# Low parts of weights started earlier and accumulated from HBM, and a top-128 search that runs on into the attention

## The chip, the cores and the metric

The kernel runs on one NeuronCore of a Trainium2 chip. The metric is the device time of one execution in microseconds. TensorE, VectorE (DVE in the profile), ScalarE (ACT), GpSimd (POOL) and SyncE (SP, which here only issues DMAs) have a queue of their own each; what one queue holds runs in order, and engines wait for each other and for DMAs by semaphores.

## The reference

Two blocks work on 512 tokens of width 1024, all in float32. The first is one layer of sparse attention: a projection of the normalized tokens to 3,432 columns, three branches over eight heads (compressed, selected and windowed keys, mixed by gates) and one branch over another eight heads that attends to the 128 best keys of an indexer:

```python
logits = jnp.einsum('bthd,bsd->bths', qi_b, ki) * (IDX_DIM ** -0.5)
score = jnp.einsum('bths,bth->bts', jax.nn.relu(logits), wi_b).astype(jnp.float32)
score = jnp.where(key_pos[None, None, :] <= t[None, :, None], score, NEG)
_, idx = lax.top_k(score, topk)            # topk = 128
```

The compressed keys come from `hid = silu(flat @ w1 + b1)` over blocks of 32 tokens. The second block has two layers; each is a mixer (a gated linear recurrence and latent attention side by side) and a feed-forward, both with a modulation that depends on a condition vector:

```python
mod = (c @ w_ada + b_ada)[:, None, :]
sh_m, sc_m, g_m, sh_f, sc_f, g_f = jnp.split(mod, 6, axis=-1)
h = rms_norm_2(x) * (1 + sc_m) + sh_m
proj = h @ w_in
...
x = x + g_m * (y @ w_out)
h = rms_norm_2(x) * (1 + sc_f) + sh_f
gate, up = jnp.split(h @ w_ffn_in, 2, axis=-1)
x = x + g_f * ((jax.nn.silu(gate) * up) @ w_ffn_out)
```

## The kernel before

Every large product is taken in the fast float32r format with two parts per operand. A weight `raw` is rounded to a high part `wh`; the low part is `wl = raw - wh`; the activations are split in the same way, and a product is three matmuls, high by high, high by low and low by high (`proj_T`, L103). So a matmul with `wl` needs the low part in SBUF.

The weights come in chunks of 128 x 1024 or fewer, in the order of a list `plan` that is written out by hand (from L296). `load_chunk` (L172) issues the load of the next chunk into one of three buffers `raw` on SyncE's queue. `split_chunk` (L185) makes the two parts. ScalarE makes `wh`. The low part is made in one of two ways, by the engine that the plan names. With `DV` VectorE subtracts. With `GP` ScalarE writes the negative rounded weight into `wl`, and a DMA issued by GpSimd adds `raw` to it (L203):

```python
act(lo[:, :n], raw[:, :n], scale=-1.0)
yield 1
nc.gpsimd.dma_start(lo[:, :n].bitcast(F32), raw[:, :n], accum_op=ALU.add)
```

`take` (L221) hands a chunk to the matmuls and starts `run_ahead` (L211), which splits up to `ahead[0]` chunks beyond it (two, at places one or none) and loads one more. There are three buffers each of `raw`, `wh` and `wl`.

The rest of the program is written as small generators that are stepped by `tick`, once for each 640 ns of estimated TensorE time, so that the operations of side jobs are emitted between the matmuls. On engines named by `order(...)` the program order is kept; in the first block up to the attention and in much of the second block that is VectorE, at places others too; in the attention it is none.

The stages are: x and the weights E (indexer columns); kv tiles, C, A, Bq and Dv (keys, queries, values), with the compression (`cmp_step`, L710), whose weights `cw1` are chunks of the plan that aren't split; the gate columns `z` (L822); the attention over 26 units (from L1089), in which the second half of `z` and the first output chunks `wo1` are woven; then, twice, mixer (`w2`, `uqr`, `uqk`, `wo2`) and feed-forward (`ffi`, `ffo`).

`best_keys` (L590) finds the 128 best keys of a token: 16 rounds of MAX8 and MATCH_REPLACE8 on VectorE for each of three query tiles (256, 384 and 512 wide); the loop at L827 ticks until every side job, these rounds too, has been emitted.

The modulation sums run on VectorE: `w_ada` comes in tiles of 128 x 512 (256 KB) and is multiplied with `c_bc` and summed along the row. `ada_first(8)` runs in the attention, `ada_first(0, 1)` beside the output projection (L1257), `ada_steps` (L1844) in the first layer's mixer and feed-forward. `enter` (L1329) starts a mixer or a feed-forward: it multiplies with unnormalized activations first, and corrects by a shift for which `shifts` (L1384) sums `raw` times the shift on VectorE.

Of the kernel before, what the change touches and what calls it, by code (L numbers as in the profile page):

```python
# [29 lines left out]
AR = 4  # L30
TICK = 640.0
# [8 lines left out]
def hybrid_kernel(ctx: ExitStack, tc: tile.TileContext, a: dict, out: bass.AP):  # L40
# [85 lines left out]
    DV, GP = nc.vector, nc.gpsimd  # L126
# [42 lines left out]
    plan = []  # L169
    loaded, ready, count = {}, {}, [0, 0, 0]  # L170

    def load_chunk(beside=None):  # L172
        i = count[0]
        if i < len(plan):
            key, l, o, n, _ = plan[i]
            raw = wpool.tile([128, 1024], F32, tag="raw", name=name("raw"), bufs=3)
            for c in (0, n // 2) if beside else (0,):
                m = n // 2 if beside else n
                nc.sync.dma_start(raw[:, c:c + m], (a[key] if l is None else a[key][l])[:, o + c:o + c + m])
                if beside:  # L180
                    beside.pop(0)()
            loaded[i] = raw
            count[0] += 1

    def split_chunk(i):  # L185
        n, e = plan[i][3:]
        raw = loaded.pop(i)
        if e is None:
            ready[i] = None, None, raw
            return  # L190
        h = wpool.tile([128, 1024], F32R, tag="wh", name=name("wh"), bufs=3)
        lo = wpool.tile([128, 1024], F32R, tag="wl", name=name("wl"), bufs=3)
        ready[i] = h, lo, raw
        if i == 0:
            for p_ in (slice(0, n // 2), slice(n // 2, n)):
                act(h[:, p_], raw[:, p_])
                tt(lo[:, p_], raw[:, p_], h[:, p_].bitcast(F32), ALU.subtract, e)
            return
        act(h[:, :n], raw[:, :n])
        if e is GP:  # L200
            act(lo[:, :n], raw[:, :n], scale=-1.0)
            yield 1
            nc.gpsimd.dma_start(lo[:, :n].bitcast(F32), raw[:, :n], accum_op=ALU.add)  # L203
        else:
            yield 2
            tt(lo[:, :n], raw[:, :n], h[:, :n].bitcast(F32), ALU.subtract, e)

    splitting = []
    ahead = [2]

    def run_ahead(i):  # L211

        yield 1
        while count[1] <= min(i + ahead[0], len(plan) - 1):
            k = count[1]
            count[1] += 1
            yield from split_chunk(k)
        if count[0] <= i + 3:
            load_chunk()

    def take(key, l, o, n):  # L221
# [6 lines left out]
        while count[0] <= i:  # L228
            load_chunk()
        while count[1] <= i:  # L230
            count[1] += 1
            finish(go(split_chunk(count[1] - 1)))
# [66 lines left out]
    def plan_n(key, cw=None, es=(DV, GP, DV, GP)):  # L299
        C = WD[key]  # L300
        for c in range(4):
            plan1(off[key] + c * 2 * C, 2 * C, es[c])
            if cw is not None:
                plan.append(("cw1", cw, c * 1024, 1024, None))
# [21 lines left out]
    for l in range(L2):  # L326
        def w2_(k, e=None):
            chunks("w2", l, 3584 + k * 1024, 1024, 1, e)

        w2_(0), w2_(1)  # L330
        for k in range(4):
            chunks("w2", l, k * 896, 896, 1, DV if k % 2 else GP)
        for p_ in range(4):
            if p_:
                w2_(2 * p_, GP), w2_(2 * p_ + 1, GP)
            if p_ == 2:
                chunks("uqr", l, 0, 1024, 1)
            if p_ == EP:
                w2_(16 + EG)
            for k in range(2):  # L340
                w2_(8 + 2 * p_ + k, DV if p_ == 2 else GP)
            for m in GB[p_]:
                if m == KD - 1:
                    chunks("uqk", l, 0, 1024)
# [3 lines left out]
        chunks("wo2", l, 3072, 1024, 5)  # L348
        for c0, n in SEGS:
            for k in range(2 * n):  # L350
                chunks("ffi", l, (2 * c0 + k) * 1024, 1024, 1, GP if c0 == 0 and 2 <= k < 5 else DV)
# [9 lines left out]
    next(xs0)  # L361
    next(xs0)
    load_chunk()
    for _ in xs0:
        pass
    nc.sync.dma_start(ident, a["cst"][:, 0:128])
# [196 lines left out]
    sco = pP.tile([128, 1152], F32, name="sco")  # L563

    def post_scores():
        for t in range(1, NT):
            W = 128 * (t + 1)
            sc = sco[:, (0, 0, 256, 640)[t]:(0, 256, 640, 1152)[t]]
# [16 lines left out]
            if t == 1:  # L585
                go(best_keys())

    masks = {}
# [120 lines left out]

    def cmp_step(s, pk):  # L710
# [3 lines left out]
        def step_(c):  # L714
# [4 lines left out]
            w = take("cw1", s, c * 1024, 1024)[2]  # L719
            for i in range(8):  # L720
# [1543 lines left out]
```

## Time and profile before

| what | value |
|---|---|
| median of 3 runs | 1773.9 us (1771.15 to 1777.37) |
| the profiled execution, its own time | 1770.79 us |
| span in the profile, first to last instruction | 1769.0 us |
| mean granted TensorE clock | 0.986 |
| TensorE busy | 95% |
| VectorE, ScalarE, GpSimd busy | 62%, 54%, 22% |
| accumulating DMAs (`wl` from `raw`) | 78 |

A page row gives the busy time of an engine, not the time in which it is at its peak. The waits name who released an engine last. The granted clock is the share of TensorE's full clock in a stretch.

### The profile page before, as it was taken

What the parts mean: (1) busy time and instruction counts of PE and PEld (TensorE: products, weight loads), DVE (VectorE), ACT (ScalarE), POOL (GpSimd) and SP (SyncE); (2) the same over time, 40 slices, a digit from 0 to 9 for tenths busy, and PEclk for the clock granted to TensorE, in tenths of its full rate; (3) what the DMA queues carried; (4) which work ended last, traced back from release to release, by engine and by line L of the source; (5) the groups of instructions that cost most, each with busy time, mean ns of one, the idle gap of its engine ahead of it and who ended that gap; (6) DMA issues with size and microseconds to landing.
All of it is one profiled execution on the core that took longest, in us unless ns stands there. A gap on an engine that the chain in (4) does not pass through costs nothing.

```text
span 1769.0 us, 22764 instructions
## 1 busy us (share of the span) xinstructions
PE 1687.9 (95%) x8122; PEld 1389.5 (79%) x8124; DVE 1103.6 (62%) x2048; ACT 958.2 (54%) x1729; POOL 381.1 (22%) x429
## 2 busy tenths in 40 slices
PE   6979899989998999999999999999999999999998
PEld 5868677667776788888888888887788888888887
DVE  5767788768689876746555546657676733333335
ACT  5558787975766786442222224887885532222223
POOL 3236344531225244100000000235243100000000
PEclk9989999999999999999999999999999999999999
DMA  6546643165787822366457443564422343333322
GB/s 199 148 125 140 150 108 84 48 177 134 189 256 209 236 49 70 98 184 226 155 190 236 149 132 94 146 146 126 124 60 72 97 129 96 96 95 98 100 86 74
DMA packets 84976, 235.91 MB, mean 133 GB/s; under 512 B 10368, under 2 KB 13056, under 8 KB 84864
## 3 DMA queue, kind: packets, MB, share of 16 engines
q1 hardware_dynamic: 73600, 194.82, 35.5%
q0 software_dynamic: 11264, 39.65, 12.1%
q8 instruction: 64, 1.05, 0.2%
q14 instruction: 48, 0.39, 0.1%
HBM read 192.69 MB, written 2.10 MB: 110 GB/s over the span
## 4 chain that ended last, share of the span: by engine, by line
PE 65%; DVE 10%; issue 9%; DMA 8%; ACT 6%; POOL 3%; SPq 0%; POOLq 0%; DVEq 0%; ACTq 0%
PE mm L84 38%; PE s L84 20%; PE o L84 3%; DMA wl<-raw 3%; DMA ada<-in_ada_dram 3%; DVE ada L1850 2%; DMA raw<-in_w_dram 2%; PE pt L930 1%; ACT p L71 1%; PE pt L2017 1%; PE pt L84 1%; DVE wl L74 1%; DVE xc L1534 1%; ACT L71 1%; DVE xl L1622 0%
## 5 line engine op out<-in xcount | busy, mean ns | idle before, releaser
L71 ACT ACTIVATE wh<-raw 128x1024 fp32r<-128x1024 f32 (+3 forms) x257 | 263.3, 1026 | 578.6 <-PE mm L84 361.7
L84 PE MATMUL mm<-hh,wh 128*128 128x512 f32 x1408 | 444.9, 393 | 3.6 <-DVE z L74 3.4
L84 PEld LDWEIGHTS mm<-hh,wh 128*128 128x128 f32 x1408 | 265.3, 189 | 58.4 <-DVE z L74 3.5
L84 PE MATMUL mm<-hh,wl 128*128 128x512 f32 x736 | 290.1, 394 | 4.6 <-DMA wl<-raw 4.5
L74 DVE TENSOR_TENSOR wl<-raw,wh 128x1024 fp32r<-128x1024 f32 (+3 forms) x179 | 213.8, 1196 | 115.9 <-ACT wh L71 113.5
L84 PE MATMUL s<-hh,wh 128*128 128x512 f32 x688 | 213.8, 390 | 0.0
L74 POOL TENSOR_TENSOR nv<-nv,pwr 128x4 f32<-128x4 f32 (+1 forms) x6 | 7.4, 1234 | 776.7 <-DVE nv L1321 432.7
L84 PEld LDWEIGHTS mm<-hh,wl 128*128 128x128 f32 x736 | 139.4, 189 | 35.3 <-DMA wl<-raw 6.5
L84 PEld LDWEIGHTS s<-hh,wh 128*128 128x128 f32 x688 | 129.4, 188 | 26.6
L84 PE MATMUL s<-hh,wl 128*128 128x512 f32 x352 | 137.8, 392 | 2.7 <-DMA wl<-raw 2.7
L84 PE MATMUL mm<-uh,wh 128*128 128x512 f32 (+1 forms) x364 | 139.2, 382 | 0.0
L84 PE MATMUL mm<-ul,wh 128*128 128x512 f32 (+1 forms) x364 | 139.0, 382 | 0.0
L84 PE MATMUL mm<-uh,wl 128*128 128x512 f32 (+1 forms) x364 | 139.0, 382 | 0.0
L203 POOL DMA_DIRECT2D wl<-raw x78 | 68.9, 887 | 254.4 <-ACT wl L71 214.8
L1850 DVE SCALAR_TENSOR_TENSOR ada<-ada,c_bc 128x512 f32<-128x512 f32 x160 | 115.8, 756 | 7.2 <-DMA ada<-in_ada_dram 7.2
L74 DVE TENSOR_TENSOR sg<-s,sg 128x512 f32<-128x512 f32 x42 | 29.1, 692 | 116.4 <-PE s L84 116.4
L71 ACT ACTIVATE p<-s,st 128x512 f32<-128x512 f32 (+3 forms) x160 | 83.9, 527 | 23.7 <-DVE st L1994 16.9
L1769 DVE SCALAR_TENSOR_TENSOR x<-mm,mod,x 128x512 f32<-128x512 f32 x46 | 34.5, 751 | 92.2 <-PE mm L84 92.2
L84 PEld LDWEIGHTS s<-hh,wl 128*128 128x128 f32 x352 | 66.4, 189 | 17.7 <-DMA wl<-raw 4.0
L84 PE MATMUL mm<-yh,wh 128*128 128x512 f32 x256 | 79.6, 392 | 0.3 <-DVE x L2119 0.3
L71 ACT ACTIVATE wl<-raw 128x1024 fp32r<-128x1024 f32 (+3 forms) x78 | 79.9, 1024 | 0.0
L84 PEld LDWEIGHTS mm<-uh,wl 128*128 128x128 f32 x364 | 68.4, 188 | 13.3
(430 smaller groups left out, 3640.7 us busy)
## 6 DMA issues: line engine op xcount, KB each, us to landing
ada<-in_ada_dram SPq DMA_DIRECT2D x192, 256.0 KB, 4.1
raw<-in_ffi_dram SPq DMA_DIRECT2D x88, 512.0 KB, 3.6
wl<-raw POOLq DMA_DIRECT2D x67, 512.0 KB, 5.4
raw<-in_w_dram SPq DMA_DIRECT2D x66, 512.0 KB, 3.9
raw<-in_ffo_dram SPq DMA_DIRECT2D x32, 512.0 KB, 3.7
raw<-in_wo_dram SPq DMA_DIRECT2D x24, 512.0 KB, 3.7
raw<-in_ffo_dram SPq DMA_DIRECT2D x16, 384.0 KB, 3.2
x<-in_xT_dram SPq DMA_DIRECT2D x16, 256.0 KB, 4.9
```

The lines of the kernel that those rows point to most:

```text
L71: nc.scalar.activation(o, i, f, **kw)
L74: (e or nc.vector).tensor_tensor(o, x, y, op)
L84: nc.tensor.matmul(o, l, r, start=start, stop=stop)
L203: nc.gpsimd.dma_start(lo[:, :n].bitcast(F32), raw[:, :n], accum_op=ALU.add)
L930: nc.tensor.transpose(tp[:n, r * 128:(r + 1) * 128], srcs[r], ident)
L1534: nc.vector.scalar_tensor_tensor(xc[:, d:], x_[:, :S - d], vec[:, j * 8 + m:j * 8 + m + 1], xc[:, d:], ALU.mult, ALU.add)
L1769: nc.vector.scalar_tensor_tensor(x[m], ps, mod[:, 40 + m:41 + m], x[m], ALU.mult, ALU.add)
L1850: nc.vector.scalar_tensor_tensor(w, w, 1.0, c_bc[:, hf * 512:(hf + 1) * 512], ALU.mult, ALU.mult, accum_out=parts[l][:, j, hf:hf + 1])
L2017: nc.tensor.transpose(tp[:, kb * 128:(kb + 1) * 128], p[:, kb * 128:(kb + 1) * 128], ident)
```

## The change

Low parts: `split_chunk` becomes two functions. `low_first` makes the low part of a `GP` chunk: the negative rounded weight by ScalarE, and an accumulating DMA whose source is now the weight in HBM. It runs three chunks ahead (`ahead[0]` is 3), with four buffers `wl`; `high` makes `wh` two chunks ahead. `raw` has two buffers. The destination of the DMA is no longer viewed as F32. Outside the feed-forwards every chunk is `GP`, but for E (two chunks by VectorE, two subtracted by GpSimd) and the first kv chunk (VectorE); the feed-forward's first five chunks are `GP`. That is 125 accumulates for 78.

The compression's weights leave the plan: `load_cw` loads them in 16 tiles of 128 x 512 into the two buffers `ada`. The shift sums of `enter` are emitted with the low part (`shift_of`). `ada_first(0)` follows `ada_first(8)` in the attention. The last search (`best_keys` of the third query tile) may run on into the attention: its scores have a buffer of their own, and the masks are finished when the first score of the third branch asks for them. The attention has nine buffers `p` for ten. `isres` is replaced by a comparison of `nres` with 0.

```diff
+RB = 2
+HB = 3
+LB = 4
...
-            raw = wpool.tile([128, 1024], F32, tag="raw", name=name("raw"), bufs=3)
+            raw = wpool.tile([128, 1024], F32, tag="raw", name=name("raw"), bufs=RB)
...
-    def split_chunk(i):
+    def low_first(i):
+        n, e = plan[i][3:]
+        while count[0] <= i:
+            load_chunk()
+        raw = loaded[i]
+        if e is GP:
+            lo = lows[i] = wpool.tile([128, 1024], F32R, tag="wl", name=name("wl"), bufs=LB)
+            act(lo[:, :n], raw[:, :n], scale=-1.0)
+            yield 1
+            nc.gpsimd.dma_start(lo[:, :n], source(i), accum_op=ALU.add)
+            if i in shift_of:
+                by_k, shift = shifts(*shift_of[i])
+                for kt in range(KD):
+                    w_ = raw[:, kt * 128:(kt + 1) * 128]
+                    if kt == 0:
+                        nc.vector.tensor_scalar(by_k, w_, shift[:, 0:1], None, ALU.mult)
+                    else:
+                        nc.vector.scalar_tensor_tensor(by_k, w_, shift[:, kt:kt + 1], by_k, ALU.mult, ALU.add)
+                    if kt % 2:
+                        yield 1
+
+    def high(i):
         n, e = plan[i][3:]
         raw = loaded.pop(i)
...
+        h = wpool.tile([128, 1024], F32R, tag="wh", name=name("wh"), bufs=HB)
+        if e is GP:
+            ready[i] = h, lows.pop(i), raw
+            act(h[:, :n], raw[:, :n])
             return
...
+            tt(lo[:, p_], raw[:, p_], h[:, p_].bitcast(F32), ALU.subtract, GP if e is SUB else DV)
...
-    ahead = [2]
+    ahead = [3]
 
     def run_ahead(i):
 
         yield 1
-        while count[1] <= min(i + ahead[0], len(plan) - 1):
-            k = count[1]
+        end = len(plan) - 1
+        while count[3] <= min(i + ahead[0] - 1, end):
+            k = count[3]
+            if count[1] <= k:
+                count[1] += 1
+                yield from low_first(k)
+            count[3] += 1
+            yield from high(k)
+        while count[1] <= min(i + ahead[0], end):
             count[1] += 1
-            yield from split_chunk(k)
-        if count[0] <= i + 3:
+            yield from low_first(count[1] - 1)
+        while count[0] <= min(i + ahead[0] + 1, end):
             load_chunk()
...
-    plan_n("E")
-    plan1(off["kv"], 1024, GP)
-    plan_n("C", 0)
+    plan_n("E", (DV, SUB, DV, SUB))
+    plan1(off["kv"], 1024, DV)
+    plan_n("C")
     plan1(off["kv"] + 1024, 1024, GP)
-    plan_n("A", 1, (GP, DV, GP, GP))
-    plan_n("Bq", None, (GP, GP, GP, GP))
-    plan_n("Dv", None, (GP, GP, GP, DV))
+    plan_n("A")
+    plan_n("Bq")
+    plan_n("Dv")
...
-            chunks("w2", l, k * 896, 896, 1, DV if k % 2 else GP)
+            chunks("w2", l, k * 896, 896, 1, GP)
...
-        chunks("wo2", l, 3072, 1024, 5)
+        chunks("wo2", l, 3072, 1024, 5, GP)
...
-    next(xs0)
-    next(xs0)
-    load_chunk()
     for _ in xs0:
         pass
+    load_chunk()
...
-                go(best_keys())
-
-    masks = {}
+                keys_p.append(go(best_keys()))
+
+    masks, keys_p = {}, []
...
+    def load_cw():
+
+        i = load_cw.n
+        if i < 16:
+            w = wpool.tile([128, 512], F32, tag="ada", name=name("cw"), bufs=AB)
+            nc.sync.dma_start(w, a["cw1"][i // 8][:, i % 8 * 512:(i % 8 + 1) * 512])
+            cws.append(w)
+            load_cw.n += 1
...
+        ahead[0] = (2, 3, 3, 3)[c]
...
-    while procs:
+    while any(p not in keys_p for p in procs):
         tick()
+    while 2 not in masks:
+        step(keys_p[0])
...
-           {"p": 10, "pth": 3, "ptl": 3, "pc": 2, "st": 5})
+           {"p": 9, "pth": 3, "ptl": 3, "pc": 2, "st": 5})
...
         if br == 2 and t:
+            finish(keys_p[0])
...
-    zs, more, ad = z_steps(), after_first(), ada_first(8)
+    def ada_both():
+        yield from ada_first(8)
+        yield from ada_first(0)
+
+    zs, more, ad = z_steps(), after_first(), ada_both()
...
-    jobs = [go(tables()), go(ada_first(0, 1))]
+    jobs = [go(tables())]
```

## Rows read from the trace of the kernel before

**Rows 1.** The page: span, busy times, and TensorE in 40 slices.

```profile
span 1769.0 us, 22764 instructions
...
PE 1687.9 (95%) x8122; PEld 1389.5 (79%) x8124; DVE 1103.6 (62%) x2048; ACT 958.2 (54%) x1729; POOL 381.1 (22%) x429
...
PE   6979899989998999999999999999999999999998
```

**Rows 2.** TensorE's waits (us, times, longest): span; 0-60; 60-190; 190-215; 370-420; 480-620.

```profile
PE mm L84 <- DMA wl<-raw: 24.0, 10, 4.8
PE pt L84 <- DMA wl<-raw: 3.7, 1, 3.7
PE s L84 <- DMA wl<-raw: 2.7, 3, 1.3
...
PE mm L84 <- DMA wl<-raw: 4.6, 1, 4.6
...
PE mm L84 <- DMA wl<-raw: 10.0, 5, 4.8
PE s L84 <- DMA wl<-raw: 1.3, 1, 1.3
...
PE mm L84 <- DVE z L74: 3.4, 1, 3.4
...
PE mm L84 <- DMA wl<-raw: 4.8, 2, 2.5
...
PE s L84 <- ACT xch L71: 4.0, 2, 3.0
PE s L84 <- DVE qkl L77: 3.6, 1, 3.6
PE mm L84 <- DMA wl<-raw: 3.2, 1, 3.2
```

**Rows 3.** Windows: stretch, length, busy time of each engine, clock, DMA share, GB/s.

```profile
60.00:190.00 130.00, 116.37 (x607) 97.26 (x607) 92.19 (x199) 93.56 (x255) 57.80 (x68) 0.96 0.59 144
190.00:215.00 25.00, 21.63 (x85) 16.70 (x84) 18.30 (x37) 14.36 (x21) 6.61 (x10) 0.86 0.78 180
215.00:290.00 75.00, 73.28 (x436) 54.77 (x434) 62.94 (x155) 59.44 (x148) 32.01 (x44) 1.00 0.39 102
290.00:370.00 80.00, 74.68 (x415) 53.91 (x417) 60.59 (x135) 70.61 (x183) 43.50 (x57) 1.00 0.22 51
380.00:400.00 20.00, 16.91 (x65) 13.29 (x66) 9.33 (x21) 10.58 (x17) 3.42 (x4) 0.91 0.95 257
480.00:620.00 140.00, 127.41 (x542) 102.31 (x541) 121.94 (x202) 96.50 (x133) 47.36 (x40) 0.96 0.80 234
```

**Rows 4.** Timeline of SyncE's, ScalarE's and GpSimd's queues before the stall at 114 us.

```profile
103.92 0.33 SPq L179 DMA_DIRECT2D raw<-in_w_dram  x1
...
110.47 1.06 ACT L71 ACTIVATE wh<-raw 128x1024 fp32r<-128x1024 f32 x1 [4.40 <-DMA raw<-in_w_dram]
...
112.77 0.86 POOL L203 DMA_DIRECT2D wl<-raw  x1 [12.99 <-ACT wl L71]
```

**Rows 5.** DMA queues, 480 to 620 us: packets, MB, share of 16 engines.

```profile
q1 hardware_dynamic: 11783, 26.92, 57.1%
q0 software_dynamic: 1580, 5.76, 22.8%
```

**Rows 6.** Groups on VectorE, 480 to 620 us: count, busy us, mean ns.

```profile
L74 DVE TENSOR_TENSOR wl<-raw,wh 128x1024 fp32r<-128x1024 f32 x10 | 13.8, 1380 | 0.0
```

**Rows 7.** Groups by shape, whole span, on GpSimd and VectorE.

```profile
L74 POOL TENSOR_TENSOR hh<-ht,hh 128x512 fp32r<-128x512 f32 x12 | 15.5, 1293 | 28.1 <-ACT ht L71 28.1
...
L1058 DVE SCALAR_TENSOR_TENSOR ada<-ada,c_bc 128x512 f32<-128x512 f32 x32 | 22.9, 719 | 15.1 <-DMA ada<-in_ada_dram 15.0
...
L601 DVE MAX8 m<-sco 128x8 f32<-128x512 f32 x16 | 11.1, 691 | 0.3
...
L602 DVE MATCH_REPLACE8 sco<-m,sco 128x512 f32<-128x512 f32 x16 | 10.8, 676 | 0.0
```

More of the change, by code (lines that the diff above doesn't have):

```diff
@@ L166, in wait, with shifts, source @@
             yield 1
-    plan = []
-    loaded, ready, count = {}, {}, [0, 0, 0]
+    plan, shift_of, shift_parts = [], {}, {}
+    loaded, lows, ready, count = {}, {}, {}, [0, 0, 0, 0]
+    def shifts(l, c0, i):
+        if i == 0:
+            shift_parts[l, c0] = pp.tile([128, 3, 128], F32, tag="wsh", name=name("wsh"), bufs=1)
+        return shift_parts[l, c0][:, i], mods[l][:, c0:c0 + 8]
+    def source(i):
+        key, l, o, n, _ = plan[i]
+        return (a[key] if l is None else a[key][l])[:, o:o + n]
     def load_chunk(beside=None):
@@ L193, in split_chunk @@
         ready[i] = h, lo, raw
[L194 to L206, printed above, removed]
+        for p_ in (slice(0, n // 2), slice(n // 2, n)) if i == 0 else (slice(0, n),):
+            act(h[:, p_], raw[:, p_])
+            if i:
+                yield 2
+            tt(lo[:, p_], raw[:, p_], h[:, p_].bitcast(F32), ALU.subtract, GP if e is SUB else DV)
@@ L347, in hybrid_kernel @@
         chunks("wo2", l, 0, 1024, 3, GP)
-        chunks("wo2", l, 3072, 1024, 5)
+        chunks("wo2", l, 3072, 1024, 5, GP)
+        shift_of.update({len(plan) + i: (l, 24, i) for i in range(3)})
         for c0, n in SEGS:
             for k in range(2 * n):
-                chunks("ffi", l, (2 * c0 + k) * 1024, 1024, 1, GP if c0 == 0 and 2 <= k < 5 else DV)
+                chunks("ffi", l, (2 * c0 + k) * 1024, 1024, 1, GP if c0 == 0 and k < 5 else DV)
             chunks("ffo", l, c0 * 1024, n * 128, KD)
@@ L562, in hybrid_kernel @@
     scores = {}
[L563 removed]
+    sco = pP.tile([128, 640], F32, name="sco")
+    sco3 = pB.tile([128, 512], F32, name="sco3")
     def post_scores():
@@ L800, in hybrid_kernel @@
     cE = dense_N("E", before_E)
-    ahead[0] = 2
+    ahead[0] = 3
     go(settled(cE, post_E))
     k0 = kv_tile(0)
+    load_cw()
+    load_cw()
     cC = dense_N("C", beside=cmp_step(0, k0))
@@ L1148, in hybrid_kernel @@
     nres = pp.tile([128, S], F32, name="nres")
-    isres = pp.tile([128, S], F32, name="isres")
     fgain = pp.tile([128, KD], F32, name="fgain")
@@ L1191, in tables @@
         yield 8
-        nc.vector.tensor_scalar(isres, posr, 0.0, None, ALU.is_equal)
-        nc.vector.tensor_scalar(nres, isres, -1.0, 1.0, ALU.mult, ALU.add)
+        nc.vector.tensor_scalar(nres, posr, 0.0, None, ALU.not_equal)
         yield 4
@@ L1381, in enter @@
         sh = pp.tile([128, 3], F32, tag="shw", name=name("shw"), bufs=2)
-        by_k = Lp.tile([128, 3, 128], F32, "F", name("wsh"))
-        def shifts(i):
-            for kt in range(KD):
-                raw = ws[i][2][:, kt * 128:(kt + 1) * 128]
-                if kt == 0:
-                    nc.vector.tensor_scalar(by_k[:, i], raw, shift[:, 0:1], None, ALU.mult)
-                else:
-                    nc.vector.scalar_tensor_tensor(by_k[:, i], raw, shift[:, kt:kt + 1], by_k[:, i], ALU.mult, ALU.add)
-                if kt % 2:
-                    yield 1
         def last(k):
@@ L1400, in enter @@
         for i in range(2):
-            ahead[0] = 2 - i
+            ahead[0] = 3
             ws.append(take(*weights[i]))
-            parts_.append(go(later(5, shifts(i))))
             w_dense(xg, ws[i], pss[i], 0, KD - 1, need=last)
@@ L1455, in w_in @@
             return "w2", l, 3584 + k * 1024, 1024
-        hs, first, need = enter(st, sc1, mod, [w_in(0), w_in(1)], POOL_IN)
+        hs, first, need = enter(st, sc1, mod, (l, 0), [w_in(0), w_in(1)], POOL_IN)
         gw = {}
@@ L1715, in layer @@
         order(mybir.EngineType.PE, mybir.EngineType.Activation)
-        hs, first, need = enter(st, sc1[:, 8:16], mod[:, 24:32], [("ffi", l, k * 1024, 1024) for k in range(3)], POOL_FF)
+        hs, first, need = enter(st, sc1[:, 8:16], mod[:, 24:32], (l, 24), [("ffi", l, k * 1024, 1024) for k in range(3)], POOL_FF)
         if l == 0:
@@ L2062, in mla @@
         yield
-        ahead[0] = 1
+        ahead[0] = 2
         yy = {}
```

59 lines of the change are left out of this document (28 added, 31 removed).

## The prediction

> **What bounds the kernel now.** I read the page's busy times first, then the list of who TensorE waited for (whole span, then stretch by stretch), the windows of those stretches, the timeline around one stall, and the DMA queues. TensorE is busy 1687.9 of 1769.0 us [rows 1], so all its idle time is 81 us. The page's row of 40 slices has a 9 for TensorE in every slice from the 14th to the last but one [rows 1]: the idle time lies mostly in the attention block and the first layer's mixer, before 620 us. The list of waits names one main cause there: matmuls wait for a low part `wl` brought by DMA, 24.0 + 3.7 + 2.7 = 30.4 us in all [rows 2]. The other waits are short chains of ScalarE and VectorE (`xch`, `qkl`, `xcl`, `z`). A stall costs twice: after it the granted clock falls to the lower of its two levels, 1.2 of 2.4 GHz, for a while, so that the mean is 0.96 in 60-190 us, 0.86 in 190-215, 0.91 in 380-400 and 0.96 in 480-620 [rows 3]. Length times what is missing to 1 gives 5.2 + 3.5 + 1.8 + 5.6 = 16 us lost to the clock, an upper bound.
>
> Why a low part is late is seen around the 4.8 us stall at 114 us [rows 2]. The load of the raw chunk is issued at 103.92; ScalarE sat idle for it until 110.47, rounded twice, and the accumulate left GpSimd at 112.77 [rows 4]. From the load's issue to the accumulate's it is 8.9 us, the accumulate still to run, and a chunk is started only two ahead; the compression's `cw1` chunks sit in the same three raw buffers.
>
> **The change, part by part.** The kernel's time in the profiled execution is 1770.8 us; the median of the runs shown is 3.1 us above it. I make the sum against the first and add 3.
>
> Opening, 0 to 60 us. The second chunk's low part is subtracted by GpSimd instead of accumulated. A 128x512 subtraction takes GpSimd 1.29 us [rows 7], so 128x696 is an estimated 1.8 us after the rounding, and the wait of 4.6 us [rows 2] should go. Against it, six x tiles are loaded ahead of the third chunk, 1.05 MB more than before. At 2.97 us per MB (below) that is 3.1 us later for a chunk needed some 4 us later. Gain between 0 and 4.6: I take 4.
>
> 60 to 190 us. The 16 `cw` loads go to buffers of their own, and low parts start three chunks ahead. The waits for low parts are 10.0 + 1.3 [rows 2], with 5.2 us of clock behind them: 16.5 at most, 0 at least. The number of accumulates here hardly changes (C gains two, A and Dv one each; E loses two, kv one). I take 12.
>
> 190 to 215 us. The one wait is for `z`, 3.4 us [rows 2], with up to 3.5 us of clock. VectorE keeps its program order, but four subtractions ahead of this place leave it (two of C, one each of A and Dv) and one, kv's, comes. Between 0 and 6.9: I take 2.
>
> Attention, 215 to 370 us. Two things come to VectorE. The first eight columns of the ada sums are 16 passes of 0.72 us, 11.5 us. A round of the 512-wide search is 0.69 + 0.68 = 1.37 us [rows 7]. Between none and all 16 rounds move in, 0 to 22 us; I take half, 11. VectorE is busy 62.9 + 60.6 = 123.5 of 155 us, and would be at 146, beside a TensorE at 148.0 [rows 3]. Queued behind a search round are the score maxima and the `ptl` subtractions, for which the transposes and the value matmuls wait. Cost between 0 and the 22.5 added; nearest to the idle time that is left, I take a loss of 4.
>
> 370 to 420 us. Here the ada loads compete with low parts: DMA share 0.95 in 380-400 [rows 3]. The loads leave for the attention, where the share is 0.39 and 0.22. The waits for low parts are 4.8, the clock 1.8; of 6.6 I take 5.
>
> 420 to 480 us. The low-part wait is 3.7 [rows 2]; the `wsh` passes are moved ahead, out of VectorE's queue at the layer's entry. I take 3.5 of it.
>
> 480 to 620 us is the place that speaks against the change. The accumulates here use 22.8% of the engines' time for 5.76 MB, so one of 0.524 MB costs 2.90 us of all 16 engines; plain loads cost 57.1% for 26.92 MB, 2.97 us per MB, 1.56 us for a chunk [rows 5]. Ten VectorE subtractions, 13.8 us [rows 6], become accumulates: 29 us more DMA on 0.80 x 140 = 112 us. That is 141 us of engine time in a stretch of 140, where TensorE is busy 127.4 [rows 3]. If the transfers ran at the 0.95 of 380-400, the stretch would take 148 us. For it speak the waits of 4.0 + 3.6 + 3.2 = 10.8 us [rows 2], most of them behind VectorE, which is relieved by 13.8 of 121.9 us. At best all 10.8 go; at the 0.95 it is 8 lost. At the share of now, 0.80, it would be 176 us, 36 lost, but that share is one of demand, not of what the engines can do. Between 10.8 won and 8 lost, nearer the full engines, I take 4 lost. The Trainium skill, page "DMA: Bandwidth & Descriptors", section "Issuing engines are not separate DMA queues", says that transfers issued by different engines run on the same 16 DMA engines and interleave. The rows agree (both queues add up to 0.80 here), so by that rule the accumulates cannot run beside the ada loads for nothing: 141 us is then a floor for this stretch.
>
> The rest: 30.4 - 4.6 - 11.3 - 4.8 - 3.7 - 3.2 = 2.8 us of low-part waits at the entries of the feed-forward and in the second layer; I take 2. In the second layer's mixer no ada loads compete. ScalarE pays 1.06 us [rows 4] for each of the 47 added roundings there and elsewhere, beside a TensorE that has the next chunks ready; I put it at nothing, and if that cover is gone it shows as waits for `wh`. GpSimd's issue, 0.86 us each [rows 4], is hidden likewise. The `isres` edit exchanges one VectorE pass for another of the same shape: nothing. Nine `p` buffers instead of ten: nothing, since scores run ahead by that many.
>
> Price of an accumulate from HBM: no row shows one. The lower end is a plain load, 1.56 us, the upper the accumulate from SBUF, 2.90, or more if the source or the conversion to float32r slows it. It is nearest to the accumulate: 2.90.
>
> Sum: 4 + 12 + 2 - 4 + 5 + 3.5 - 4 + 2 = 20.5 us. 1770.8 - 20.5 = 1750.3, and with 3 for the median, 1753.
>
> **The rivals.** A: the DMA engines become the bound in the first layer's mixer. If low parts and ada data come late in turn, VectorE, in program order, stands before an ada sum. At 20 us lost rather than 4 the time is 1769. The shares of 0.95 and 0.80 speak for it, the three chunks of lead against it.
>
> B: the raw load takes the place of the low part. With two raw buffers a load waits until the chunk two before it is rounded, so ScalarE waits for raw data as it did at 110.47 [rows 4], and the low-part waits stay as before save the opening and the `cw` one (4 + 4.8). The change would then not do what it says; 1774 - 8 = 1766.
>
> C: VectorE becomes the bound in the attention: 20 us lost instead of 4, 1769. For it, 146 of 155 us busy; against it, that the mask is first needed when the third branch starts.
>
> D, the other sign: the accumulate itself is dearer. At twice 2.90, the 21 low parts of 480-620 us need 122 us beside 80 of plain loads, 202 in place of 140: 62 lost there. Set against some 25 won elsewhere that is 1774 + 37 = 1811, or more with the second layer. It decides from 21 X + 80 = 140 + 25, X = 4.0 us. Against it: nothing in the rows makes HBM a slow source. The same page, section "SWDGE vs HWDGE vs iDMA", states that a float32r destination always casts; the kernel before bitcasts to F32 and the changed one does not. No row here shows a casting transfer, and the page gives it no price.
>
> **How the numbers follow.** My forecast 0.60 (its own range 1733 to 1765); A 0.13, B 0.08, C 0.09, D 0.10. This kernel's measurement can tell about 0.3%, 5.3 us. Faster holds my forecast and about half of A, B and C, some beyond the edge on either side: 0.72; same 0.15; slower 0.13, D with the tail of A. If every low-part wait, the clock behind them and the short chains went, it would be 1773.9 - 30.4 - 16 - 3.4 - 7.6 = 1716; I let the range begin at 1728. At the top, A and C together give 1785; I end it at 1780, which leaves out D and little else.
>
> **What would show it.** Right: low-part waits of TensorE fall from 30 us to under 8; the stall at 13 us, those of 100-130 and that at 437 are gone, and the clock is 1.0 there; 125 accumulates, at about 2.9 us of engine time. Wrong: DMA shares near 1.0 in 480-620 with VectorE waiting for `ada`; ScalarE waiting for `raw`; TensorE idle in the attention behind VectorE.

## The result and the profile after

The changed kernel takes 1784.83 us (median of 4 runs, 1782.80 to 1788.44), the kernel before 1772.81 beside it (1771.15 to 1777.37): a ratio of 1.0072, with an interval of 1.0049 to 1.0095. It is 12 us slower; 1753 and a gain were predicted.

The page of the changed kernel (line numbers are its own: a matmul is L87, a rounding L74, an accumulate L209), beside [rows 1]: span and busy times; of the 40 slices PE, ACT and DMA; under them the DMA queues (packets, MB, share of 16 engines):

```profile
span 1783.5 us, 22792 instructions
...
PE 1697.5 (95%) x8124; PEld 1392.2 (78%) x8124; DVE 1055.2 (59%) x1998; ACT 1009.9 (57%) x1783; POOL 415.6 (23%) x478
...
PE   7999999899898799999999999899999999999998
...
ACT  6579878866876776542222225788886542232223
...
DMA  7767532376898824756556535777723733333332
...
q1 hardware_dynamic: 74752, 194.82, 34.2%
q0 software_dynamic: 18032, 63.98, 21.3%
```

Beside [rows 2], TensorE's waits over the whole span (us, times, longest), and under them ScalarE's largest sum of waits for raw loads and, in 480 to 620 us, VectorE's for ada data:

```profile
PE s L87 <- ACT p L74: 7.8, 8, 2.9
PE s L87 <- ACT xch L74: 7.0, 4, 3.3
...
PE pt L1689 <- DVE lat L1541: 6.3, 4, 2.2
PE mm L87 <- DMA wl<-in_w_dram: 5.0, 3, 2.5
PE s L87 <- ACT qkh L74: 4.6, 2, 4.3
...
PE mm L87 <- DMA wl<-in_wo_dram: 2.1, 1, 2.1
...
PE s L87 <- DMA wl<-in_ffi_dram: 2.0, 2, 1.2
...
ACT wl L74 <- DMA raw<-in_w_dram: 43.4, 25, 4.2
...
DVE ada L1891 <- DMA ada<-in_ada_dram: 23.6, 11, 3.9
```

The waits for low parts fell from 30.4 us [rows 2] to 9.1, nearly as forecast, and the kernel is slower all the same: TensorE now waits longer for ScalarE (`p`, `xch`, `qkh`) and VectorE (`lat`). Of the 14.5 us by which the span grew, 9.6 are busy time of TensorE (1697.5 against 1687.9) for the same matmuls, and 4.9 are idle time. Before the change, VectorE's wait for ada data in 480 to 620 us and ScalarE's two largest sums for raw loads were

```profile
DVE ada L1850 <- DMA ada<-in_ada_dram: 7.2, 5, 3.1
...
ACT wh L71 <- DMA raw<-in_w_dram: 17.9, 9, 4.7
...
ACT wh L71 <- DMA raw<-in_ffo_dram: 8.8, 2, 4.4
```

The windows of the changed kernel beside [rows 3], and the queues of 480 to 620 us beside [rows 5]:

```profile
60.00:190.00 130.00, 122.26 (x645) 101.53 (x644) 103.23 (x227) 107.60 (x272) 63.97 (x77) 1.00 0.71 162
...
290.00:370.00 80.00, 68.26 (x341) 49.34 (x340) 58.86 (x144) 66.66 (x154) 37.35 (x43) 0.94 0.32 88
...
480.00:620.00 140.00, 121.48 (x500) 95.95 (x499) 102.14 (x182) 97.74 (x132) 49.76 (x47) 0.94 0.94 257
```

```profile
q1 hardware_dynamic: 11064, 25.39, 51.3%
q0 software_dynamic: 2880, 10.49, 42.0%
```

60 to 190 us holds 6 us more of busy TensorE, at a clock of 1.00; the attention's end and the first layer's mixer hold 6 us less each.

Averages over fixed windows shift with the kernel, so I followed the start of the same matmuls through the timelines. The table gives when each starts, in us of the one profiled execution of each kernel (for the last of the compression, when its last row of matmuls starts); the last four columns are experiments told below.

| matmul | before | changed | cw_and_opening | raw3_sbuf_alternate | raw3_sbuf | raw3 |
|---|---|---|---|---|---|---|
| last of the compression | 136.0 | 119.8 | 113.5 | 115.0 | 114.3 | 117.0 |
| first value matmul | 221.4 | 197.5 | 195.5 | 191.7 | 191.3 | 197.0 |
| last value matmul | 363.8 | 357.9 | 338.8 | 349.4 | 349.1 | 357.7 |
| last of the output projection | 413.1 | 401.4 | 389.4 | 391.1 | 390.7 | 404.0 |
| first `lat` transpose, layer 1 | 465.4 | 456.0 | 441.6 | 441.8 | 442.9 | 457.2 |
| first `qkh` score, layer 1 | 608.1 | 608.6 | 585.5 | 589.5 | 595.4 | 607.9 |
| first `uh` matmul, layer 1 | 826.5 | 828.1 | 804.4 | 814.4 | 819.0 | 840.5 |
| first `lat` transpose, layer 2 | 1144.8 | 1154.8 | 1122.7 | 1135.5 | 1143.1 | 1165.9 |
| last `uh` matmul, layer 2 | 1758.7 | 1773.3 | 1736.7 | 1756.8 | 1765.6 | 1796.3 |

The changed kernel leads by 24 us at the first value matmul, by 6 at the last, by 9 at the first `lat` transpose, by nothing at the first layer's scores, loses 8 more (1154.8 - 828.1 against 1144.8 - 826.5) up to the second layer's `lat` and 5 behind it. These are single traces: two of the kernels below, alternate and ada_back, have the changed kernel's code up to the attention and start the first value matmul at 202.8 and 205.7 us, 19 and 16 ahead of before. So a gain ahead of the attention is there, near the 18 forecast (16 to 24), and it is lost in several places.

### The profile page after: what moved, and what is told of

Same layout as the page of the kernel before. It is cut to its first block, busy times and chain, and to the rows that moved or that the text cites. A ratio compares the mean times of both kernels' runs of the same rounds, so it can differ in the third digit from the quotient of the medians.

```text
span 1783.5 us, 22792 instructions
## 1 busy us (share of the span) xinstructions
PE 1697.5 (95%) x8124; PEld 1392.2 (78%) x8124; DVE 1055.2 (59%) x1998; ACT 1009.9 (57%) x1783; POOL 415.6 (23%) x478
## 3 DMA queue, kind: packets, MB, share of 16 engines
q0 software_dynamic: 18032, 63.98, 21.3%
## 4 chain that ended last, share of the span: by engine, by line
PE 64%; DMA 9%; ACT 9%; DVE 8%; issue 7%; POOL 3%; SPq 0%; DVEq 0%; ACTq 0%; POOLq 0%
PE mm L87 39%; PE s L87 19%; DMA raw<-in_w_dram 4%; PE o L87 3%; DMA ada<-in_ada_dram 2%; ACT wl L74 1%; PE pt L988 1%; ACT wh L74 1%; PE pt L2058 1%; DMA wl<-in_ffi_dram 1%; DVE ada L1891 1%; ACT R L74 1%; DMA raw<-in_ffi_dram 1%; ACT L74 1%; DVE xc L1575 1%
## 5 line engine op out<-in xcount | busy, mean ns | idle before, releaser
L74 ACT ACTIVATE wh<-raw 128x1024 fp32r<-128x1024 f32 (+3 forms) x257 | 263.3, 1025 | 504.2 <-PE mm L87 344.8
L87 PE MATMUL mm<-hh,wh 128*128 128x512 f32 x1408 | 444.9, 394 | 5.0 <-DVE z L77 2.6
L87 PEld LDWEIGHTS mm<-hh,wh 128*128 128x128 f32 x1408 | 265.4, 189 | 61.0 <-issue 3.0
L87 PE MATMUL mm<-hh,wl 128*128 128x512 f32 x736 | 288.9, 393 | 4.3 <-DMA wl<-in_w_dram 4.3
L77 DVE TENSOR_TENSOR wl<-raw,wh 128x1024 fp32r<-128x1024 f32 (+2 forms) x130 | 152.7, 1175 | 114.2 <-ACT wh L74 111.9
L87 PE MATMUL s<-hh,wh 128*128 128x512 f32 x688 | 214.7, 391 | 0.0
L209 POOL DMA_DIRECT2D wl<-in_w_dram x81 | 71.5, 886 | 594.1 <-ACT wl L74 550.3
L74 ACT ACTIVATE wl<-raw 128x1024 fp32r<-128x1024 f32 (+2 forms) x125 | 129.3, 1034 | 76.4 <-DMA raw<-in_w_dram 43.4
L87 PEld LDWEIGHTS mm<-hh,wl 128*128 128x128 f32 x736 | 139.0, 189 | 34.6 <-DMA wl<-in_w_dram 5.1
L87 PEld LDWEIGHTS s<-hh,wh 128*128 128x128 f32 x688 | 129.6, 189 | 27.3 <-POOL hh L77 0.2
L87 PE MATMUL mm<-uh,wh 128*128 128x512 f32 (+1 forms) x364 | 139.2, 382 | 0.0
L87 PE MATMUL mm<-ul,wh 128*128 128x512 f32 (+1 forms) x364 | 139.0, 382 | 0.0
L87 PE MATMUL mm<-uh,wl 128*128 128x512 f32 (+1 forms) x364 | 139.0, 382 | 0.0
L87 PE MATMUL s<-hh,wl 128*128 128x512 f32 x352 | 138.1, 392 | 0.0
L74 ACT ACTIVATE p<-s,st 128x512 f32<-128x512 f32 (+3 forms) x160 | 83.7, 526 | 22.8 <-DVE st L2035 13.6
L87 PE MATMUL mm<-yh,wh 128*128 128x512 f32 x256 | 79.6, 392 | 0.7 <-DVE x L2160 0.7
L87 PEld LDWEIGHTS mm<-uh,wl 128*128 128x128 f32 x364 | 68.4, 188 | 13.4
L87 PEld LDWEIGHTS mm<-ul,wh 128*128 128x128 f32 x364 | 68.4, 188 | 13.3
```

The lines of the kernel that those rows point to most:

```text
L74: nc.scalar.activation(o, i, f, **kw)
L77: (e or nc.vector).tensor_tensor(o, x, y, op)
L87: nc.tensor.matmul(o, l, r, start=start, stop=stop)
L209: nc.gpsimd.dma_start(lo[:, :n], source(i), accum_op=ALU.add)
```

## The experiments

The theories to begin with: 1, ScalarE's added roundings stand in its queue and wait there for raw data that comes late (rival B); 2, the DMA engines are full (rival A); 3, VectorE in the attention (rival C). Theory 4, an accumulate that lands late, came up with the first runs. Ratios are to the kernel before, with 95% intervals; in the code, `...` marks what is left out.

**Raw buffers and division of the work.** raw3, on the changed kernel:

```diff
-RB = 2
+RB = 3
...
-LB = 4
+LB = 3
...
-        while count[1] <= min(i + ahead[0], end):
+        while count[1] <= min(i + ahead[0] - 1, end):
```

> The changed kernel with its low parts begun two chunks ahead in three buffers, and the buffer so freed given to the raw chunks, of which there are three again. Theory 1 (ScalarE's added roundings stand in its queue before raw data that has too short a lead, and what is queued behind them is late for TensorE): ScalarE's waits for raw loads fall from 65 us to under 25, the 13 us lost at the second layer's entry and some of the 10 in the first layer's mixer come back, 1765 to 1770 us in place of 1785; low-part waits of TensorE may rise from 9 to 15. Theory 2 (the accumulates fill the DMA engines in the first layer's mixer): DMA share stays near 1.0 there, raw waits stay, 1782 to 1788. Theory 3 (VectorE in the attention, from the search and the ada sums moved in): nothing of the 10 us lost in the attention comes back here, whatever the rest does.

Measured: 1806.42 us, 1.0198 (1.0175 to 1.0221). ScalarE's waits for raw loads fell from 77.4 us (all rows; the 65 of the expectation are the three largest) to 10.7, the three rows here, and TensorE's waits for low parts rose to 50 us:

```profile
ACT wh L74 <- DMA raw<-in_ffo_dram: 8.8, 2, 4.4
...
ACT wl L74 <- DMA raw<-in_w_dram: 1.0, 1, 1.0
...
ACT wh L74 <- DMA raw<-in_w_dram: 0.9, 1, 0.9
```

The kernel became 22 us slower, outside what either theory gave. So an end of the waits for raw data doesn't pay for a shorter lead. What those waits cost by themselves isn't shown: a kernel with three raw buffers and the lead of three was not run.

alternate, on the changed kernel; two of its lines are shown, the other chunks of the second block go back in the same way, except those that feed the shift sums:

```diff
-            chunks("w2", l, k * 896, 896, 1, GP)
+            chunks("w2", l, k * 896, 896, 1, DV if k % 2 else GP)
...
-        chunks("wo2", l, 3072, 1024, 5, GP)
+        chunks("wo2", l, 3072, 1024, 5)
```

> The changed kernel with the low parts of the second block divided between VectorE subtractions and accumulates as before the change (the four chunks that feed the shift sums stay accumulates); buffers and lead stay as changed. Theory 2 (the DMA engines are full, or ScalarE carries too many roundings): the DMA share in the first layer's mixer falls to 0.85 or less, its 10 us and the second layer's 13 us come back, 1762 to 1767 us. Theory 1 (two raw buffers): fewer early roundings but the same raw buffers, so about half comes back, 1772 to 1776. Theory 3: the first layer's attention stays as slow as in the changed kernel, first MLA score of the first layer not earlier than 598.

Measured: 1776.84 us, 1.0040 (1.0022 to 1.0059): 8 us come back, fewer than theory 2 gave. all_accumulate is the reverse on the kernel before, for the second block outside the feed-forwards:

> The kernel before with one part of the change alone: all low parts of the second block outside the feed-forward by accumulate (source in SBUF, two ahead, three raw buffers). Theory 2: slower by 10 to 23 us, 1783 to 1796, with the DMA share near 1.0 in the first layer's mixer and VectorE waiting for ada data. Theory 1: three raw buffers keep ScalarE supplied, so within 5 us of before, 1769 to 1778.

Measured: 1788.80 us, 1.0108 (1.0080 to 1.0136), 16 us slower, with three raw buffers. In 480 to 620 us its accumulates take 39.8% of the engines (the queue's row), and VectorE waits for ada data as in the changed kernel (the row of waits):

```profile
q0 software_dynamic: 2843, 10.34, 39.8%
```

```profile
DVE ada L1850 <- DMA ada<-in_ada_dram: 30.9, 10, 7.7
```

So these accumulates cost 8 to 16 us. Theory 2, that they do so by filling the engines, fits all_accumulate: there the share rises from 0.80 to 0.92, and the stretch from the first `lat` transpose to the first `qkh` score from 142.7 to 154.2 us. It doesn't fit what the changed kernel loses in that stretch. alternate between these two matmuls (columns as in [rows 3]):

```profile
460.40:612.20 151.80, 137.30 (x567) 109.06 (x566) 125.45 (x221) 100.80 (x137) 48.20 (x42) 0.94 0.75 218
```

The DMA share is 0.75, less than the 0.78 of the kernel before there, and the stretch still takes 151.8 us, where the changed kernel takes 152.6 at a share of 0.91. The 8 us come back behind it. Both edits also change the number of ScalarE's roundings, so these runs don't tell the engines' part from ScalarE's.

**The source of the accumulate.** from_hbm, on the kernel before:

```diff
-            nc.gpsimd.dma_start(lo[:, :n].bitcast(F32), raw[:, :n], accum_op=ALU.add)
+            key, l, o, _, _ = plan[i]
+            nc.gpsimd.dma_start(lo[:, :n], (a[key] if l is None else a[key][l])[:, o:o + n], accum_op=ALU.add)
```

> The kernel before with the accumulates reading the raw chunk from HBM and casting to float32r, nothing else. It measures the price: 512 KB cost 2.83 us of all 16 engines from SBUF before and 3.11 in the changed kernel. If source and cast make that difference, 3.0 to 3.2 here with 78 accumulates, 20 us more engine time over the span; if crowding did, 2.8 to 2.9. Time: theory 1 says a raw buffer is free earlier, 0 to 4 us faster; theory 2 says dearer transfers in the full stretch, 0 to 4 slower. A rise of over 20 us would revive the rival of a dear accumulate.

cast_only leaves away only `.bitcast(F32)` and keeps `raw` as the source:

> The kernel before with the destination of the accumulates written as float32r and nothing else; the source stays the raw chunk in SBUF. Reading from HBM and casting together made the kernel before 31.9 us slower, with the landing of an accumulate at 8.0 us in place of 5.4. Theory 4a (the source in HBM makes the accumulate late): landing 5.4 to 5.8 us, time within 5 us of before. Theory 4b (the cast does): landing near 8, 20 to 32 us slower.

from_hbm: 1804.68 us, 1.0175 (1.0149 to 1.0200), 32 us slower by this one edit. cast_only: 1773.85 us, 1.0000 (0.9983 to 1.0017). The queue of the accumulates and their issues (times, KB each, median us from issue to landing) on the page of from_hbm, and then on that of before:

```profile
q0 software_dynamic: 11264, 39.65, 12.4%
...
wl<-in_w_dram POOLq DMA_DIRECT2D x41, 512.0 KB, 8.0
...
wl<-in_wo_dram POOLq DMA_DIRECT2D x14, 512.0 KB, 7.5
```

```profile
q0 software_dynamic: 11264, 39.65, 12.1%
...
wl<-raw POOLq DMA_DIRECT2D x67, 512.0 KB, 5.4
```

The engines' time per 512 KB hardly rises: 0.124 x 1803.3 / 39.65 x 0.524 = 2.96 us, 2.83 before. The landing rises from 5.4 us to 8.0 for the chunks of the largest group, and TensorE's waits for low parts from 30.4 us to 53.8. In cast_only the landing is 5.4 as before. The Trainium skill, page "DMA: Bandwidth & Descriptors", section "SWDGE vs HWDGE vs iDMA", says that a float32r destination always casts. By cast_only such a cast from SBUF costs nothing here, so the source is what does; a read from HBM without the cast was not run.

from_sbuf puts the accumulate's line of before, with `raw` as the source, into the changed kernel:

> The changed kernel with its accumulates reading the raw chunk in SBUF, as before the change; lead, buffers and plan stay as changed, so a raw buffer is held until its accumulate has landed. Theory 4 (the accumulate from HBM lands later, and the longer lead only pays for it): 10 to 20 us faster than the changed kernel, 1765 to 1775, unless theory 1 eats it: with two raw buffers held longer, ScalarE's waits for raw data rise above 65 us and the time is 1785 or more.

Measured: 1841.97 us, 1.0387 (1.0364 to 1.0409). Low parts are no longer late (2.4 us of waits), but a raw buffer is now held until the accumulate has landed, and ScalarE stands for it (138.6 us over all rows, 77.4 in the changed kernel):

```profile
PE mm L87 <- DMA wl<-raw: 2.4, 2, 1.3
...
ACT wl L74 <- DMA raw<-in_w_dram: 88.7, 36, 6.4
...
ACT wl L74 <- DMA raw<-in_ffi_dram: 18.5, 6, 5.8
```

So with two raw buffers the accumulate had better read HBM, and theory 1 is a real cost once it does not. raw3_sbuf has raw3's buffers and lead, and the accumulate's line of before, which reads SBUF:

> As raw3 (three raw buffers, low parts begun two ahead in three buffers), and the accumulates read the raw chunk in SBUF again. Only the source differs from raw3, which took 1806. Theory 4 (the accumulate from HBM lands 2.5 us later, and the longer lead pays for that and no more): 25 to 33 us faster than raw3, 1773 to 1781, accumulates landing at 5.4 to 5.8 us. If not the source but the two-chunk lead cost raw3 its 22 us, it stays at 1800 or more.

Measured: 1778.80 us, 1.0033 (1.0019 to 1.0047): 27.6 us faster than raw3 by that line, whose view as F32 cast_only put at nothing. The accumulates land at 5.6 in place of 7.5 us (raw3, then raw3_sbuf):

```profile
q0 software_dynamic: 18032, 63.98, 20.4%
...
wl<-in_w_dram POOLq DMA_DIRECT2D x65, 512.0 KB, 7.5
```

```profile
q0 software_dynamic: 18032, 63.98, 19.7%
...
wl<-raw POOLq DMA_DIRECT2D x109, 512.0 KB, 5.6
```

From raw3 the changed kernel then differs by four low buffers, two raw ones and a lead of three, which give 1806.4 - 1784.8 = 21.6 us. The lead pays back most of what the source costs, and no more: 6 us are lost.

**The attention.** ada_back takes `ada_first(0)` out of the attention (`jobs = [go(tables()), go(ada_first(0, 1))]`); search_first issues the search to its end ahead of it (`while procs: tick()`). Both on the changed kernel:

> The changed kernel with the first eight columns of the ada sums back beside the output projection, out of the attention. Between the first value matmul and the last the changed kernel took 18 us longer than before. If VectorE's 16 ada passes are what is late there (theory 3, ada), 8 to 15 of them come back, and 370 to 420 us loses up to 5 again: 1772 to 1780. If the search is (theory 3, search), the attention stays as long, 1783 to 1790.

> The changed kernel with the top-128 search issued to its end before the attention begins. Theory 3, search: the attention is 8 to 15 us shorter than in the changed kernel, and the stretch ahead of it up to 10 longer, 1774 to 1782. Theory 3, ada: no gain in the attention and up to 10 us lost ahead of it, 1785 to 1795. If neither changes the attention's end, what is lost there was never gained ahead of it, because the attention's own chain of ScalarE sets its end.

ada_back: 1782.09 us, 1.0055 (1.0036 to 1.0074), not clear of the changed kernel; first to last value matmul is 9 us shorter than there (151.2 against 160.4, before 142.4), 12 us are lost again from there to the first `lat` transpose, and 5 come back in the mixer. search_first: 1784.79 us, 1.0065 (1.0040 to 1.0089), no change. Groups on VectorE, first of before and then of the changed kernel: the search by tile (duration, first and last start), and the ada passes between the first and the last value matmul (count, busy us, mean ns):

```profile
L601 DVE MAX8 m<-sco x48: 404/561/696, 59.3 to 203.5; 128x8 f32<-128x256 f32 x16, 128x8 f32<-128x384 f32 x16, 128x8 f32<-128x512 f32 x16
...
L1058 DVE SCALAR_TENSOR_TENSOR ada<-ada,c_bc 128x512 f32<-128x512 f32 x16 | 11.7, 732 | 0.0
```

```profile
L637 DVE MAX8 m<-sco x48: 404/560/697, 57.1 to 187.8; 128x8 f32<-128x256 f32 x16, 128x8 f32<-128x384 f32 x16, 128x8 f32<-128x512 f32 x16
...
L1116 DVE SCALAR_TENSOR_TENSOR ada<-ada,c_bc 128x512 f32<-128x512 f32 x32 | 27.7, 864 | 1.1 <-DMA ada<-in_ada_dram 1.1
```

The last search round starts at 187.8, ahead of the first value matmul at 197.5, as it does in the kernel before (203.5 and 221.4): no round of the search runs beside the value matmuls. Only ada passes moved in, 32 where there were 16. What makes the other 9 of the 18 us, the nine `p` buffers for one, no run here separates.

**Building up from the gain.** cw_and_opening is the kernel before with two parts of the change: the compression's loads out of the plan, in buffers of their own, and the opening.

```diff
-    plan_n("E")
-    plan1(off["kv"], 1024, GP)
-    plan_n("C", 0)
+    plan_n("E", None, (DV, SUB, DV, SUB))
+    plan1(off["kv"], 1024, DV)
+    plan_n("C")
...
-            w = take("cw1", s, c * 1024, 1024)[2]
+                w = cws[i // 4]
```

> The kernel before with two parts of the change alone: the compression's loads in buffers of their own and out of the chunk plan, and the opening (second and fourth chunk subtracted by GpSimd, kv by VectorE, the x tiles ahead of the third chunk). These were put at 4 for the opening and most of 12 for 60 to 190 us in the prediction. If they make the 16 us that the changed kernel gains by the last compression matmul, that matmul is 10 to 16 us earlier than 136.0 and the whole is 5 to 14 us faster than before, 1760 to 1768; if the longer lead makes them, within 4 us of before.

Measured: 1751.62 us, 0.9882 (0.9863 to 0.9901), faster than both kernels, and by more than expected. The table shows where: 22.5 us by the last compression matmul, and no loss behind it. Its waits for low parts and its 60 to 190 us:

```profile
PE mm L84 <- DMA wl<-raw: 8.5, 6, 2.5
PE pt L84 <- DMA wl<-raw: 3.4, 1, 3.4
PE s L84 <- DMA wl<-raw: 1.3, 2, 0.7
```

```profile
60.00:190.00 130.00, 124.81 (x651) 103.73 (x651) 103.65 (x219) 102.66 (x266) 64.17 (x75) 0.99 0.66 162
```

cw_only has the compression's loads alone:

> The kernel before with the compression's loads in buffers of their own alone, the opening as before. The two together gained 21 us, 22.5 of them by the last compression matmul. If the opening made 4 of these as the prediction put it, this one is 15 to 19 us faster than before, 1754 to 1758; if the opening made 10, 1762; if the opening is worth nothing, 1751 to 1753.

Measured: 1760.32 us, 0.9921 (0.9905 to 0.9937). These loads make 13.4 us, the opening the other 8.7. TensorE's waits of cw_only in the first 140 us suggest why the opening is worth more than its one stall:

```profile
PE mm L84 <- DMA wl<-raw: 6.0, 1, 6.0
...
PE pt L513 <- ACT R L71: 5.9, 2, 5.0
```

Behind the low part stands a second stall, of 5.0 us for `R` at 39 us (at 38 in the kernel before); with the opening the waits for `R` there are 1.5 us.

raw3_sbuf_alternate is raw3_sbuf with alternate's edit; raw3_sbuf_attention is that with the attention of before:

> As raw3_sbuf, and the second block's low parts divided between VectorE and accumulates as before the change (the chunks of the shift sums stay accumulates). What is left of the change is the compression's loads in buffers of their own, the opening, the first block's accumulates, the attention's edits and the moved shift passes. Theory: the division gave 8 us on the changed kernel and all accumulates cost 16 on the kernel before, so 1762 to 1770; the second layer's entry loses 0 to 3 us in place of 8; the attention still loses 10.

> As raw3_sbuf_alternate, and the attention as before the change: ada sums beside the output projection, search ended ahead of the attention, ten score buffers. If the ada sums are a loss in the attention that comes back only in part (9 of 18 us there, 8 given back by the first lat transpose), within 4 us of raw3_sbuf_alternate; if the gain ahead of the attention survives it, 1760 to 1768.

Measured: 1770.63 us, 0.9988 (0.9976 to 1.0000), and 1775.06 us, 1.0010 (0.9998 to 1.0022). Both are a little outside what was expected. Here the attention of before is 4.4 us slower than the changed one (by the intervals of the two ratios, 1 to 7); and 19 us lie between cw_and_opening and raw3_sbuf_alternate. Five kernels add one part each to cw_and_opening:

> cw_and_opening (1752) with four more low parts of the first block by accumulate, as the change has them (two of C, one each of A and Dv). If VectorE's subtractions were late there, 2 to 5 us faster, 1747 to 1750; if accumulates are late for TensorE wherever they are added, 2 to 6 slower, 1754 to 1758.

> cw_and_opening with the low parts of the chunks that feed the shift sums (two at each mixer's entry, two more at each feed-forward's) by accumulate, as the change has them; the shift passes stay where they were. If the accumulates at the entries make the loss that raw3_sbuf_alternate has there (1771, some 13 us lost at the five entries and mixers behind the attention), 5 to 13 slower, 1757 to 1765; if moving the passes or the lead does, within 4 us of 1752.

> cw_and_opening with the attention's edits of the change: search run on into it, both ada sums in it, third score tile kept, nine score buffers. If these are a loss (theory 3: 18 us in the attention, 14 given back around it), 2 to 8 slower, 1754 to 1760, with value matmuls ending 10 to 15 us later relative to the first; if the stretch around them pays it back in full, within 3 of 1752.

> cw_and_opening (1752) with the changed kernel's order of a chunk's work: for an accumulated chunk the negated rounding and the accumulate first and the high part behind them, and raw loads up to four chunks ahead in the three buffers; nothing else. First block's accumulates, shift chunks and attention together explain 0 + 4.5 + 3.4 of the 19 us between cw_and_opening and raw3_sbuf_alternate. If this order makes the other 11, 1759 to 1763; if the moved passes do, 1750 to 1754.

> cw_and_opening with the shift passes moved as in the change: made from the raw chunk beside its accumulate, two chunks ahead of its use, with the low parts of these chunks by accumulate and the lead of two kept at the entries (and the one mask tile less that makes room for it). The accumulates alone took 4.5 us. If the moved passes make the 11 us that are left, 1763 to 1768, most of it in the second layer's mixer; if the order does, 1754 to 1758.

| kernel | us | against 1751.6 | ratio to before |
|---|---|---|---|
| plus_first_accumulate | 1751.88 | +0.3 | 0.9875 (0.9856 to 0.9895) |
| plus_shift_accumulate | 1756.17 | +4.6 | 0.9902 (0.9878 to 0.9925) |
| plus_attention | 1755.04 | +3.4 | 0.9895 (0.9878 to 0.9911) |
| plus_order | 1752.72 | +1.1 | 0.9889 (0.9869 to 0.9909) |
| plus_moved_passes | 1763.93 | +12.3 | 0.9949 (0.9931 to 0.9967) |

By the intervals of the ratios, a difference between two of these kernels is known to some 5 us either way. So the first four rows are not clear of zero, and only the last one is. It holds plus_shift_accumulate's edit, so the moved passes, with the `isres` edit and the lead kept at two at the entries, where it was two and then one, are 7.8 (3 to 13). Windows of 1080 to 1140 us, the second layer's entry, in plus_moved_passes and then in plus_shift_accumulate (busy time as in [rows 3]):

```profile
sum 60.00, PE 57.05 PEld 47.09 DVE 39.68 ACT 43.79 POOL 16.48; mean PE 57.05 PEld 47.09 DVE 39.68 ACT 43.79 POOL 16.48
```

```profile
sum 60.00, PE 59.98 PEld 51.26 DVE 39.79 ACT 49.67 POOL 18.51; mean PE 59.98 PEld 51.26 DVE 39.79 ACT 49.67 POOL 18.51
```

TensorE loses 3 us there, in waits of 1 us or less each for VectorE, GpSimd and a low part. Followed by matmul, plus_moved_passes is 7 us behind plus_shift_accumulate at the end of the output projection, 3 at the first `qkh` score, 7 at the second layer's first `lat` and 10 at the end. Which queue the passes hold up was not settled. Nor do the parts quite add up: 0.3 + 4.6 + 3.4 + 1.1 + 7.8 = 17.2 of 19.0.

## Why the prediction was wrong

By medians, from the kernel before to the changed one (a minus is faster): the compression's loads -13.4, the opening -8.7, first block's accumulates +0.3, attention +3.4, accumulates of the shift chunks +4.6, moved shift passes +7.8, order +1.1, not assigned +1.8, all other low parts of the second block by accumulate +8.2 (raw3_sbuf less raw3_sbuf_alternate), the source in HBM +27.6, the lead with its buffers -21.6. Together +11.1; 12.0 was measured, beside other runs of the kernel before. These are the steps of one way from kernel to kernel, so they have to add up, and another order of steps could give other sizes. Clear of noise are the first two, the moved passes, the 8.2 and the last two.

- **The step that failed first is the price of an accumulate from HBM, "It is nearest to the accumulate: 2.90".** As engine time that is nearly right: 140 x 0.420 / 10.49 x 0.524 = 2.94 us in 480 to 620, and 0.213 x 1783.5 / 63.98 x 0.524 = 3.11 over the span. But TensorE doesn't wait for engine time, it waits for the landing, and that went from 5.4 to 8.0 us in from_hbm, which cost 32 us. The 12 us for 60 to 190 us counted the longer lead as a gain, where it had a later landing to pay for first: the two together lose 27.6 - 21.6 = 6.0. Rival D had the sign and the transfer; its point of decision, 4.0 us of engine time, was never reached, since it too priced only the engines.
- **The term with the largest error is 420 to 480 us, +3.5 with the `wsh` passes moved ahead.** Its low-part wait fell only from 3.7 to 1.8 us, and the moved passes with the accumulates of their chunks cost 12.3 us over the whole of plus_moved_passes, the second layer's entries included. I had credited one entry with VectorE's shorter queue, and not costed the same edit at the three other entries.
- **60 to 190 us and the opening**: 12 and 4 forecast, 13.4 and 8.7 measured when alone. The loads' own buffers make the first, not the lead; the opening's term left out the stall for `R` behind the low part. In the changed kernel 16.2 us remain by the last compression matmul (raw3_sbuf: 21.7); what takes the rest was not settled.
- **190 to 215 us** was put at +2. The wait for `z` [rows 2] is still there, 2.6 us at 179 us; no run here separates this term.
- **Attention and 370 to 420 us**: -4 and +5 forecast, together a gain of 1. Of the 11 us of search that were to move in none did; the 16 ada passes did. First to last value matmul took 14 us longer in plus_attention than in cw_and_opening, and 8 of these came back by the first `lat` transpose. The same edits were a loss of 3.4 there, not clear of noise, and a gain of 4.4 in raw3_sbuf_alternate, so their sign in the changed kernel is not known. Rival C's place was right, its cause half so and its size, for the whole, too large.
- **480 to 620 us, 4 lost**: between the same two matmuls, first `lat` to first `qkh`, the changed kernel lost 9.9 and all_accumulate 11.5. In all_accumulate the mechanism was right and the size too small. In the changed kernel it isn't shown: alternate lost 9.1 there with the engines at 0.75. What else slows that stretch stays open; in both, TensorE's clock is lower there, 0.95 and 0.94 against 0.99 before. The changed kernel's two queues add up to 93.3% in 480 to 620 us. The Trainium skill (page "DMA: Bandwidth & Descriptors", section "Issuing engines are not separate DMA queues") says that DMAs run on the same 16 engines whichever engine started them, and the sum agrees.
- **ScalarE's 47 roundings at nothing**: `wh` was never the wait. TensorE waits for `xch`, `qkh` and `p` instead, which share ScalarE's queue with the roundings; 77.4 us of waits for raw data stand in it, 29.9 before. In raw3 this cost went and low parts were late; in from_sbuf it grew and they were not. What the roundings and these waits cost by themselves was not measured.
- Right were the accumulates (125), the clock of 1.00 in 60 to 190, nearly so the waits for low parts (9.1, forecast under 8), and the signs of failure named for rivals A and B both appeared. That the waits for low parts went as forecast while the time did not shows that they alone were no measure of it.

## What to carry to other kernels

A DMA has two prices: the engines' time, which counts where they are full, and the time to landing, which counts where someone waits; a change of its source has to be costed in both. A longer lead is a gain only after it has paid for what made it possible: here a third raw buffer was given for it, which forced the source into HBM. A pass that is moved has to be costed at every place where it moves. And a change of many parts is best run part by part, since 22 us of gain were hidden under 33 of loss: the compression's loads and the opening alone make 1751.6 us, the fastest kernel measured here.

## What was not expected of the hardware

An accumulating DMA of 512 KB that reads HBM lands at 8.0 us (median) where the one that reads SBUF lands at 5.4, in otherwise the same kernel, while the engines' time for it grows only from 2.83 to 2.96 us; in raw3 against raw3_sbuf it is 7.5 against 5.6, and 3.02 against 2.87. Why the landing grows by more than the packets' time was not tried. A destination in float32r, so with a cast, changed neither the landing (5.4) nor the time (1.0000) where the source was SBUF.
